# Splitting the first load of a row-variance kernel into 16 and 112 partitions

## The chip, the cores and the metric

The kernel runs on one core of one Trainium2 chip. The metric is the device time of one execution in microseconds (us); three runs of the kernel before the change had a median of 164.93 us (164.89 to 165.06).

## The reference

The input `x` is 32 x 512 rows of 1024 float32 numbers, 67.1 MB in all. For each row the kernel returns the mean of the squares minus the square of the mean, a single float32.

```python
def reference(x: np.ndarray) -> np.ndarray:
    mean_sq = np.mean(x**2, axis=-1)
    sq_mean = np.mean(x, axis=-1)**2
    return (mean_sq - sq_mean).astype(np.float32)
```

## The kernel before

The 16,384 rows are laid out as 128 partitions times 128 columns: partition p holds rows 128p to 128p + 127, each row being one "column" of 1024 elements. Sixteen columns make a tile. A tile is loaded by one DMA that brings 16 neighbouring rows, 64 KB (65,536 bytes) contiguous in memory, into each of the 128 partitions: 8.39 MB. Three slots in SBUF hold tiles in turn (`slots`, `SLOTS = 3`).

All loads go out on SyncE (SP), through the helper `load` at line 124 of the profile. `load` first puts waits for the slot to be free on SP (line 123) and then the DMA, which adds 16 to its semaphore when it has landed. The order is written out by hand:

- six main tiles (`MAIN`), one DMA each. Tiles 0, 1 and 2 fill the three slots with nothing to wait for; tile t from 3 on waits until VectorE (DVE) and ScalarE (ACT) are done with tile t - 3 (`freed`).
- the last two tiles in a taper of ever smaller DMAs (`TAPER`, 11 columns down to 1) and five pieces of half and quarter columns (`PIECES`).

Of a main tile, ten or eleven columns are taken by DVE, two `bn_stats` of 512 elements each (lines 128 and 130), and the other five or six by ACT, a Square and a Copy pass with an accumulator each (line 139). Both engines wait for the semaphore of the tile before their first column and for nothing else of the loads. GpSimd (POOL) folds the statistics into variances (lines 155 to 189) when a group is complete. The last pieces go through `bn_stats` and `bn_aggr` on DVE (lines 302 and 307), and one DMA stores all 16,384 results.

The kernel allocates its semaphores itself and runs inside one critical section. After the program is built, `move` takes the load of tile 0 (all DMAs whose names are in `early`) out of the section and puts it at the very start of SP's program, ahead of the barrier in which all engines meet (line 365 in the profile); the wait for the store is put at the end. The places that the change touches are the list `rows` in the loop over tiles, which names the partition ranges in which tile 0 is loaded, and what follows from it: one `load` for each entry, one name in `early` for each, and `landed = (tile_sems[t], 16 * len(rows))`, the value for which DVE and ACT wait.

Of the kernel before, what the change touches and what calls it, by code (L numbers as in the profile page):

```python
# [10 lines left out]
P = 128  # L11
# [27 lines left out]
    (127, 768, 256),  # L39
]  # L40

class Stream:
# [24 lines left out]
def kernel(  # L70
# [8 lines left out]
    def src(c, n, e0=0, elems=D, p0=0, np=P):  # L79
        return dataclasses.replace(  # L80
            xf,
            offset=(p0 * NCOLS + c) * D + e0,
            ap=[[NCOLS * D, np], [1, (n - 1) * D + elems]],
        )
# [27 lines left out]
    def slot(t):  # L112
        return slots[t % SLOTS]

    def column(t, j, e0=0, n=D):
        return slot(t)[:, j * D + e0 : j * D + e0 + n]
# [4 lines left out]
    def load(dst, source, sem, *waits):  # L121
        for s, v in waits:
            nc.sync.wait_ge(s, v)  # L123
        return nc.sync.dma_start(out=dst, in_=source).then_inc(sem, 16)  # L124

    def bn_column(stats, xcol, *waits):
        dve.issue(
            lambda: nc.vector.bn_stats(out=stats[:, 0, :], in_=xcol[:, 0:HALF]), *waits  # L128
        )
        return lambda: nc.vector.bn_stats(out=stats[:, 1, :], in_=xcol[:, HALF:D])  # L130
# [14 lines left out]
    def act_column(xcol, c, *waits):  # L145
        act_pass(xcol, ACTF.Square, 1.0 / 32.0, msq[:, c : c + 1], *waits)
        act_pass(xcol, ACTF.Copy, 1.0 / D, mv[:, 0, c : c + 1])
# [45 lines left out]
    with tc.tile_critical(no_gpsimd_drain=True):  # L193
# [4 lines left out]
        freed = []  # L198
        for t in range(MAIN):
            if t == 0:  # L200
                rows = [(0, P)]
            else:
                rows = [(0, P)]
            waits = freed[t - SLOTS] if t >= SLOTS else ()
            for p0, np in rows:
                ins = load(
                    slot(t)[p0 : p0 + np, :],
                    src(t * SLOT, SLOT, p0=p0, np=np),
                    tile_sems[t],
                    *waits,  # L210
                )
                if t == 0:
                    early.append(ins.ins.name)
            landed = (tile_sems[t], 16 * len(rows))
            first_d = first_a = (landed,)
            n_bn = MAIN_BN - (t < SPARE)
            for j in range(SLOT):
                if j < n_bn:
                    last = bn_column(stats_main[:, t * MAIN_BN + j], column(t, j), *first_d)
                    first_d = ()  # L220
                    if j == n_bn - 1:
                        dve.step(last)
                    else:
                        last()
                else:
                    act_column(column(t, j), t * SLOT + j, *first_a)
                    first_a = ()
            freed.append((dve.done(), act.done()))
# [141 lines left out]
```

## Time and profile before

| | |
|---|---|
| median of 3 runs | 164.93 us (164.89 to 165.06) |
| the profiled execution | 164.89 us |
| its span, first to last instruction | 162.4 us |
| what lies around the span | 2.5 us |
| DVE busy | 103.0 us (63%) |
| ACT busy | 91.7 us (56%) |
| POOL busy | 12.3 us (8%) |
| DMA, share of 16 engines' span | 96.7% on SP's queue |
| HBM read | 67.11 MB, 414 GB/s over the span |

Busy times overlap each other, as do consecutive instructions of one engine. Of the DMA there is one share for all 16 DMA engines together, and the bytes that they moved. In the tables by stretch a DMA packet is counted, with its bytes and its time, in the stretch in which it starts; one packet of a main tile's load is one partition's 64 KB. A very short stretch can therefore show a share far above 1 and a rate that no engine has: it says how many packets started there.

### The profile page before, as it was taken

The page shows a single profiled execution, that of the slowest core. Times are in us where ns is not written, and L with a number is a line of the kernel's source. Part 1 is how long each engine was busy: PE and PEld are TensorE (multiplying, and loading weights), DVE is VectorE, ACT ScalarE, POOL GpSimd, SP SyncE. Part 2 cuts the span into 40 slices and gives each one's busy share as a digit, 9 for nine tenths or more (in the row PEclk, how much of TensorE's full clock was granted, in tenths as well). Part 3 has the DMA queues.
Part 4 walks back from the last instruction along what each step waited for, and adds up shares of the span by engine and source line. Part 5 has one row for each costly group of instructions (what it writes and reads, how often), then busy time and mean ns, then how long its engine had stood idle before and what let it go on. Part 6 is the DMA issues. An engine that isn't in the chain of part 4 may idle for free.

```text
span 162.4 us, 476 instructions
## 1 busy us (share of the span) xinstructions
DVE 103.0 (63%) x175; ACT 91.7 (56%) x173; POOL 12.3 (8%) x51
## 2 busy tenths in 40 slices
DVE  0000049940799208993199913998059999999983
ACT  3000049960799308960199403992059939987990
POOL 0000000000000000000000000000000048300172
DMA  8998997997997998998998999899799999999980
GB/s 274 500 468 355 468 484 339 468 500 339 452 517 339 438 517 357 420 517 371 404 517 371 404 517 404 371 517 436 339 444 444 433 390 438 429 424 410 405 317 16
DMA packets 2738, 67.19 MB, mean 414 GB/s; under 512 B 304, under 2 KB 688, under 8 KB 1328
## 3 DMA queue, kind: packets, MB, share of 16 engines
q1 hardware_dynamic: 2736, 67.18, 96.7%
q14 instruction: 2, 0.02, 0.0%
HBM read 67.11 MB, written 0.07 MB: 414 GB/s over the span
## 4 chain that ended last, share of the span: by engine, by line
DMA 78%; DVE 10%; ACT 8%; SPq 2%; issue 0%
DMA slot<-in_x_dram 78%; ACT scratch L139 8%; DVE stats_main L128 4%; DVE stats_main L130 4%; SPq L124 2%; DVE stats_end L302 2%; DVE mv L307 0%; SPq L365 0%; SPq L123 0%; SPq L193 0%
## 5 line engine op out<-in xcount | busy, mean ns | idle before, releaser
L139 ACT ACTIVATE scratch<-slot 128x1024 f32<-128x1024 f32 x86 | 86.7, 1008 | 65.6 <-DMA slot<-in_x_dram 65.5
L128 DVE BATCH_NORM_STATS2 stats_main<-slot 128x6 f32<-128x512 f32 x64 | 43.4, 679 | 56.0 <-DMA slot<-in_x_dram 56.0
L130 DVE BATCH_NORM_STATS2 stats_main<-slot 128x6 f32<-128x512 f32 x64 | 43.3, 677 | 0.0
L139 ACT ACTIVATION_READ_ACCUMULATOR scratch<-slot 128x1 f32 x86 | 16.1, 187 | 0.0
L155 POOL TENSOR_TENSOR sqm<-mv 128x2 f32<-128x2 f32 (+3 forms) x8 | 1.6, 201 | 142.2 <-ACT scratch L139 142.2
L128 DVE BATCH_NORM_STATS2 stats_late<-slot 128x6 f32<-128x512 f32 x17 | 11.6, 682 | 0.4 <-DMA slot<-in_x_dram 0.2
L130 DVE BATCH_NORM_STATS2 stats_late<-slot 128x6 f32<-128x512 f32 x17 | 11.5, 677 | 0.0
L302 DVE BATCH_NORM_STATS2 stats_end<-slot 128x6 f32<-128x512 f32 (+1 forms) x5 | 2.7, 569 | 0.3 <-DMA slot<-in_x_dram 0.3
L139 ACT ACT_TABLE_LOAD x1 | 1.3, 1283 | 0.9 <-SPq L193 0.9
L156 POOL TENSOR_TENSOR mv<-msq,sqm 128x2 f32<-128x2 f32 (+3 forms) x8 | 1.6, 202 | 0.6
L130 DVE BATCH_NORM_STATS2 stats_end<-slot 128x6 f32<-128x512 f32 x2 | 1.4, 676 | 0.0
L128 DVE BATCH_NORM_STATS2 stats_end<-slot 128x6 f32<-128x512 f32 x2 | 1.3, 668 | 0.0
L189 POOL TENSOR_SCALAR mv<-qsb_late 128x7 f32<-128x7 f32 (+3 forms) x4 | 0.8, 238 | 0.1
L172 POOL TENSOR_TENSOR q_main<-stats_main 128x264 f32<-128x264 f32 x1 | 0.6, 642 | 2.1 <-DVE stats_main L130 2.1
L166 POOL TENSOR_TENSOR msa_main<-stats_main 128x132 f32<-128x132 f32 x1 | 0.6, 595 | 0.0
L166 POOL TENSOR_TENSOR vsa_main<-stats_main 128x132 f32<-128x132 f32 x1 | 0.6, 577 | 0.0
L307 DVE BATCH_NORM_AGGREGATE mv<-stats_end 128x2 f32<-128x12 f32 (+1 forms) x2 | 0.5, 225 | 0.1
L274 DVE BATCH_NORM_AGGREGATE mv<-stats_end 128x2 f32<-128x12 f32 x2 | 0.4, 211 | 0.1
L166 POOL TENSOR_TENSOR qsa_main<-q_main 128x132 f32<-128x132 f32 x1 | 0.4, 406 | 0.1
L178 POOL TENSOR_SCALAR msb_main<-msb_main 128x66 f32<-128x66 f32 x1 | 0.4, 404 | 0.1
L182 POOL TENSOR_SCALAR qsb_main<-qsb_main 128x66 f32<-128x66 f32 x1 | 0.4, 395 | 0.1
L189 POOL TENSOR_SCALAR mv<-qsb_main 128x66 f32<-128x66 f32 x1 | 0.4, 385 | 0.1
(23 smaller groups left out, 5.4 us busy)
## 6 DMA issues: line engine op xcount, KB each, us to landing
slot<-in_x_dram SPq DMA_DIRECT2D x1, 5632.0 KB, 38.8
slot<-in_x_dram SPq DMA_DIRECT2D x1, 3584.0 KB, 28.0
slot<-in_x_dram SPq DMA_DIRECT2D x1, 2560.0 KB, 33.7
slot<-in_x_dram SPq DMA_DIRECT2D x1, 1536.0 KB, 36.9
slot<-in_x_dram SPq DMA_DIRECT2D x1, 1024.0 KB, 38.9
slot<-in_x_dram SPq DMA_DIRECT2D x2, 512.0 KB, 40.1
slot<-in_x_dram SPq DMA_DIRECT2D x3, 256.0 KB, 40.6
slot<-in_x_dram SPq DMA_DIRECT2D x2, 128.0 KB, 28.6
```

The lines of the kernel that those rows point to most:

```text
L124: return nc.sync.dma_start(out=dst, in_=source).then_inc(sem, 16)
L128: lambda: nc.vector.bn_stats(out=stats[:, 0, :], in_=xcol[:, 0:HALF]), *waits
L130: return lambda: nc.vector.bn_stats(out=stats[:, 1, :], in_=xcol[:, HALF:D])
L139: lambda: nc.scalar.activation(out=row, in_=xcol, func=func, scale=scale, accum_out=accum),
L155: w = pool.step(lambda: tt(out=sqm, in0=mean, in1=mean, op=ALU.mult), *waits)
L156: pool.step(lambda: tt(out=var, in0=meansq, in1=sqm, op=ALU.subtract), w)
L166: lambda: tt(out=a, in0=v[:, :, 0:2], in1=v[:, :, 2:4], op=ALU.add), *waits
L172: w = pool.step(lambda: tt(out=q, in0=mean, in1=mean, op=ALU.mult), *waits)
L178: lambda: ts(out=ms, in0=ms, scalar1=0.25, scalar2=None, op0=ALU.mult), w
L189: lambda: ts(out=var, in0=qs, scalar1=1.0 / D, scalar2=None, op0=ALU.mult),
L302: lambda: nc.vector.bn_stats(out=stats[:, s, :], in_=dst), (piece_sems[i], 16)
L307: lambda: nc.vector.bn_aggr(out=mv[:, :, c], in_=stats[:, 0:s, :]), w
```

## The change

Tile 0 is loaded by two DMAs in place of one. The first brings the 16 columns of partitions 0 to 15 (1.05 MB), the second those of partitions 16 to 127 (7.34 MB). Both stand at the start of SP's program, ahead of the entry barrier, and both add 16 to the same semaphore, so that DVE and ACT wait for 32 instead of 16. Every other DMA and every instruction of the other engines is the same, in the same order.

```diff
@@ -39,7 +39,7 @@
     (127, 768, 256),
 ]
 
-
+FIRST = 16
 
 
 class Stream:
@@ -198,7 +198,7 @@
         freed = []
         for t in range(MAIN):
             if t == 0:
-                rows = [(0, P)]
+                rows = [(0, FIRST), (FIRST, P - FIRST)]
             else:
                 rows = [(0, P)]
             waits = freed[t - SLOTS] if t >= SLOTS else ()
```

## The prediction

> **What bounds the kernel now.** I read the page first, its slices and its chain.
>
> ```profile
> span 162.4 us, 476 instructions
> DMA  8998997997997998998998999899799999999980
> GB/s 274 500 468 355 468 484 339 468 500 339 452 517 339 438 517 357 420 517 371 404 517 371 404 517 404 371 517 436 339 444 444 433 390 438 429 424 410 405 317 16
> DMA 78%; DVE 10%; ACT 8%; SPq 2%; issue 0%
> ```
>
> The sixteen DMA engines are busy in every slice up to the last one or two, and 78% of the chain that ended last is loads of x. Where the chain runs through ACT (24 passes) or DVE, it follows the release of a slot back, not a stage in which the loads stood still. The waits, asked next, say the same from the engines' side:
>
> ```profile
> ACT scratch L139 <- DMA slot<-in_x_dram: 65.5, 9, 20.2
> DVE stats_main L128 <- DMA slot<-in_x_dram: 56.0, 6, 22.4
> DVE stats_end L302 <- DMA slot<-in_x_dram: 0.3, 1, 0.3
> DVE stats_late L128 <- DMA slot<-in_x_dram: 0.2, 1, 0.2
> ```
>
> DVE waits for a load at each of the six main tiles, 56.0 us together, and only 0.5 us after that. So up to the landing of tile 5 the loads set the pace, and then DVE keeps step with them.
>
> How a load runs is read from stretches cut for it: the start, the second row of each engine, and whole tiles.
>
> ```profile
> core 0: us, DVE busy (x) ACT busy (x) POOL busy (x), PEclk, DMA share, GB/s
> 0.00:0.90 0.90, 0.00 (x0) 0.00 (x0) 0.19 (x4) 1.00 0.00 0
> 0.90:1.10 0.20, 0.00 (x0) 0.16 (x1) 0.12 (x2) 1.00 6.09 1966
> 1.10:1.30 0.20, 0.00 (x0) 0.20 (x1) 0.04 (x1) 1.00 2.97 983
> 1.30:1.50 0.20, 0.00 (x0) 0.20 (x1) 0.00 (x0) 1.00 1.06 328
> 1.50:1.70 0.20, 0.00 (x0) 0.20 (x1) 0.00 (x0) 1.00 1.02 328
> 1.70:1.90 0.20, 0.00 (x0) 0.20 (x1) 0.00 (x0) 1.00 4.94 1638
> 1.90:3.90 2.00, 0.00 (x0) 0.32 (x1) 0.00 (x0) 1.00 0.00 0
> 3.90:6.40 2.50, 0.00 (x0) 0.00 (x0) 0.00 (x0) 1.00 0.97 419
> 22.40:41.70 19.30, 11.97 (x20) 12.58 (x24) 0.00 (x0) 1.00 1.00 435
> ```
>
> A packet counts where it starts. 1966 GB/s for 0.2 us is 0.393 MB, six packets of 64 KB; the next stretches hold 3, 1, 1 and 5, sixteen in all, then 2 us without a start, then 419 GB/s x 2.5 us = 1.05 MB, sixteen again. So each of 16 engines takes one partition's 64 KB at a time, one after the other. In steady running (22.4 to 41.7) they move 435 GB/s, 27.2 GB/s each: **one partition's 64 KB takes 2.41 us**, and a tile, eight partitions an engine, 19.3 us. Their first packets start over 0.9 us, between 0.9 and 1.9.
>
> **The change, part by part.**
>
> *The second issue on SP.* One more DMA issue stands ahead of the entry barrier. The issue instructions of line 124 last 0.33 to 0.44 us where nothing holds them up. On SP three things are behind it: its part in the barrier, tile 1's issue (at 0.98 us now) and all later loads. SP waits 0.7 us at line 365 for the others anyway, which covers it. Without that cover, tile 1's issue would come at 1.4, and its packets are wanted when tile 0's are through, near 20 us; DVE and ACT, released by the barrier, have nothing to do before 22.4. Cost: nothing, 0.4 us if it fell on the path. The wait for 32 instead of 16 costs nothing by itself: it is the same wait, ended by the later landing.
>
> *The 16-partition DMA.* It is sixteen packets of 64 KB, as many as the engines. The trace of before has no load on fewer than 128 partitions, so its price needs bounds. If the 2.41 us belong to the engine, sixteen engines take a packet each side by side: 2.41 us, the same as those rows cost now. If they belong to the way into a group of partitions, sixteen neighbouring partitions may reach only a few of the sixteen ways. The one ratio that the trace has is eight partitions to an engine: if those eight were neighbours with one way of their own, 16 partitions would be two ways, eight packets after one another on each: 19.3 us, so 16.9 us lost. Between the ends lie four ways (4 x 2.41 = 9.6 us, 7.2 lost) and eight ways (4.8 us, 2.4 lost). Below nothing is possible too: see the first rival. I take **four ways, +7.2 us**: the row that bears on it, eight partitions to an engine, points to the two-way end, and I go one halving away from it because the groups need not be of eight neighbours.
>
> Here the Trainium skill speaks against the change. "SBUF — State Buffer", section "Door 1: The DMA port swizzle", says that DMA rate depends on how many of 16 ports the partitions reach, that partitions 0 to 15 reach four, and gives 104 GB/s for 1 MiB on them. By that figure the first DMA would take an estimated 10.1 us and the sum would be about 173 us from this step alone; by the steady row of this trace, read as the engine's own, it would be unchanged. No run of before shows which.
>
> *The 112-partition DMA.* Seven packets an engine, 7 x 2.41 = 16.9 us if all sixteen run side by side; with the first DMA that is eight packets an engine, as now, so the low bound is 0. But if ways into partitions count, those that the first DMA did not use still have all their eight packets to take: 19.3 us, one packet time more. And with seven partitions an engine, shares no longer line up with groups of eight: in the worst case two engines share a way throughout, 16.9 us more. I take the value nearest to the steady row, which has eight packets on a way: **+2.4 us**.
>
> *Does it reach the end?* Between tiles the only thing DVE and ACT wait for is the load; DVE sits idle 6.2 to 7.6 us before the start of tiles 1 to 5. Tiles 1 and 2 stand in the same queue behind tile 0 and come later by as much. Slot 0 is free by the same amount later, but tile 3's DMA lies queued for long before it is served: the six main loads take 45.2 us from issue to landing, of which 19.3 is work. So a delay of tile 0 moves all landings, the taper and the tail as a block. The same holds for a gain.
>
> *Sum.* The profiled execution took 164.89 us, 162.4 of span and 2.5 around it, 0.04 under the median of 164.93. 164.9 + 0 + 7.2 + 2.4 = **174.5 us**.
>
> **The rivals.**
>
> *Faster: the engines start together.* Now the sixteen engines start over 0.9 us, and the landing of the tile is that of the last one. If the spread comes from laying out eight packets an engine, one packet each cuts it to an eighth, 0.11 us, and the last engine gains 0.8; if it comes from elsewhere, 0. Middle of the upper half: 0.6 us, **164.3 us**. It decides if the 2.41 us belong to the engine: then the 16-partition DMA has no price, and any gain at the start is left over. For it: sixteen separate starts, a late group of five at 1.7 to 1.9, and a rate that is the same for every packet. Against it: a steady 16 x 27.2 GB/s in loads over all partitions cannot tell engine and way apart. Chance 0.25.
>
> *Two ways, or heavy sharing in the second DMA.* Two ways give +16.9, with one packet time more +19.3: 181.8 to **184.2 us**. Four ways with 4 to 5 packet times lost in the 112-partition DMA come to the same. For it: the ratio of eight to an engine. Against it: it needs the worst layout. Chance 0.2.
>
> *Nothing moves.* Engine-bound packets and a start spread that the split leaves alone: **164.9 us**. The bytes, the engines and the order are the same, so this is what the change not doing what it says looks like. Chance 0.05.
>
> *Only the issue costs.* Engine-bound, but the second DMA's packets come 0.4 us late or its engines restart: **165.3 us**. Against it: the first DMA's 2.41 us cover the 0.4. Chance 0.05.
>
> **How the numbers follow.** The forecast case, a few ways shared, has 0.45; its own range goes from eight ways and nothing more (167.3) to four ways and two packet times (177). Faster 0.25, same 0.05, slower 0.45 + 0.2 + 0.05 = 0.70; 0.2% (0.33 us) is about what a measurement of this kernel can tell from no change. The range starts at the largest gain, 164.1, since the faster case alone is more than may be left out, and ends at 183, inside the two-way case, with some 0.1 above it.
>
> **What would show it.** In the changed profile the 16-partition DMA takes near 10 us to land rather than 3 to 4, the rate in the first 10 us falls to a quarter of 435 GB/s, DVE's first wait goes from 22.4 to near 32 us, and all later landings shift by the same 9.6 us with 19.3 us between them. It is wrong if the second sixteen packets start at 3.9 to 6.4 us as now: then the engine sets the rate, and what is left is the start. If the gap between the first and second landing is not 19.3 us, the engines were left uneven, and the 112-partition term is mis-sized.

## The result, and the profile after

The changed kernel takes **185.59 us** (median of 4 runs, 185.47 to 185.84) where the kernel before takes 165.0 (4 runs, 164.89 to 165.1): the ratio is 1.125, with a 95% interval of 1.1231 to 1.127. It is 20.6 us slower. The forecast was 174.5 us, and its range ended at 183: the sign was right, the size was not. The profiled execution has a span of 183.3 us against 162.4.

The page of the changed kernel, the lines that answer to those shown of before:

```profile
span 183.3 us, 477 instructions
DMA  9199999977899999998899999999899999999970
GB/s 229 29 200 229 343 300 229 229 229 329 386 458 443 458 458 458 431 443 388 372 443 443 458 458 458 443 415 415 386 429 452 442 391 423 425 426 403 409 286 17
DMA 71%; ACT 14%; DVE 9%; another core or an unknown queue 4%; SPq 2%; issue 0%
```

Read the share and the GB/s line together. The share of the DMA engines is as high as before, 96.7% over the span, but in the first nine slices (4.6 us each) they move some 200 to 340 GB/s in place of 435. They are not idle. Their packets last longer. (The single 1 and the 29 in the second slice come from counting a packet where it starts.) From the twelfth slice on the rate is that of before. The chain has more of ACT, whose 24 passes it now follows in two tiles, and a 6.7 us piece, from 56.3 to 63.05 us, that it could not place; tile 1's load was running then.

The waits:

```profile
ACT scratch L139 <- DMA slot<-in_x_dram: 86.1, 9, 41.0
DVE stats_main L128 <- DMA slot<-in_x_dram: 77.1, 6, 43.7
DVE stats_end L302 <- DMA slot<-in_x_dram: 0.3, 1, 0.3
DVE stats_late L128 <- DMA slot<-in_x_dram: 0.2, 1, 0.2
```

DVE's longest wait, the one for tile 0, went from 22.4 to 43.7 us. The sum went from 56.0 to 77.1, so the other five waits together are as they were (33.6 and 33.4), and so is the 0.5 us after them. The whole loss is in the landing of tile 0, and it is passed on as a block: the taper's first column starts on DVE at 153.77 us against 132.74, 21.0 later.

The start, in stretches that are cut at the packets' starts:

```profile
core 0: us, DVE busy (x) ACT busy (x) POOL busy (x), PEclk, DMA share, GB/s
0.90:1.90 1.00, 0.00 (x0) 0.49 (x1) 0.15 (x2) 1.00 8.51 1049
1.90:8.70 6.80, 0.00 (x0) 0.80 (x1) 0.00 (x0) 1.00 0.00 0
8.70:10.50 1.80, 0.00 (x0) 0.00 (x0) 0.00 (x0) 1.00 3.10 583
10.50:14.70 4.20, 0.00 (x0) 0.00 (x0) 0.00 (x0) 1.00 0.00 0
14.70:43.30 28.60, 0.00 (x0) 0.00 (x0) 0.00 (x0) 1.00 1.01 259
43.70:63.00 19.30, 11.97 (x20) 12.58 (x24) 0.00 (x0) 1.00 1.00 435
```

1049 GB/s for 1 us and 583 for 1.8 are sixteen packets of 64 KB each: the first packets (the 16-partition DMA) start between 0.9 and 1.9 us, and the second ones between 8.7 and 10.5. In a row with sixteen starts, one for each engine, the share times the row's length is the mean time of one packet: 8.5 us for the first packets, 5.6 for the second. The row with 259 GB/s also counts the first packets of tile 1; up to 39.7 us, without them, it is 252. Before, the second ones started between 4.0 and 5.2:

```profile
1.90:4.00 2.10, 0.00 (x0) 0.32 (x1) 0.00 (x0) 1.00 0.00 0
4.00:5.20 1.20, 0.00 (x0) 0.00 (x0) 0.00 (x0) 1.00 2.03 874
5.20:20.00 14.80, 0.00 (x0) 0.00 (x0) 0.00 (x0) 1.00 0.98 425
```

So the 16-partition DMA cost the last engine 5.3 us (10.5 against 5.2), and the 112-partition DMA the rest: 43.7 - 10.5 = 33.2 us against 22.4 - 5.2 = 17.2, **16.0 us more**. 5.3 + 16.0 = 21.3, the shift of the landing. From 43.7 on a tile takes 19.3 us at 435 GB/s again.

### The profile page after: what moved, and what is told of

Its sections match the earlier page's. It is cut to its first block, busy times and chain, and to the rows that moved or that the text cites. A ratio compares the mean times of both kernels' runs of the same rounds, so it can differ in the third digit from the quotient of the medians.

```text
span 183.3 us, 477 instructions
## 1 busy us (share of the span) xinstructions
DVE 102.9 (56%) x175; ACT 91.7 (50%) x173; POOL 12.3 (7%) x51
## 3 DMA queue, kind: packets, MB, share of 16 engines
q1 hardware_dynamic: 2752, 67.18, 96.7%
## 4 chain that ended last, share of the span: by engine, by line
DMA 71%; ACT 14%; DVE 9%; another core or an unknown queue 4%; SPq 2%; issue 0%
DMA slot<-in_x_dram 71%; ACT scratch L139 14%; DVE stats_main L128 4%; DVE stats_main L130 4%; SPq L124 2%; DVE stats_end L302 1%; DVE mv L307 0%; SPq L123 0%
## 5 line engine op out<-in xcount | busy, mean ns | idle before, releaser
L128 DVE BATCH_NORM_STATS2 stats_main<-slot 128x6 f32<-128x512 f32 x64 | 43.4, 678 | 77.1 <-DMA slot<-in_x_dram 77.1
```

## The experiments

Theory A is that partitions reach SBUF through sixteen ways of limited rate, that a DMA over part of the partitions reaches only some of them or lets two engines meet on one, and that the sharing is the whole loss. In every kernel but one, marked below, the load of tile 0 is the only thing that differs from the kernel before. "Before" beside them was 164.88 to 165.04 us. Where no ratio is given, the time is that of one execution.

**Two DMAs, split by columns.**

```diff
-                rows = [(0, P)]
+                rows = [(0, 2), (2, SLOT - 2)]
...
-                    slot(t)[p0 : p0 + np, :],
-                    src(t * SLOT, SLOT, p0=p0, np=np),
+                    slot(t)[:, k0 * D : (k0 + nk) * D],
+                    src(t * SLOT + k0, nk),
```

> Tile 0 in two DMAs, but split by columns: 2 of 16 columns for all 128 partitions, then 14 columns for all 128. Theory A (what costs is that 16 neighbouring partitions, and seven-partition shares after them, share few ways into SBUF): no such sharing, so 165.0 us, within 0.4 us either way. Rival B (what costs is a second DMA for the same tile, a restart or a completion between the two): most of the 20.6 us stays, 180 us or more. If the first engines' starts come closer together, a gain of up to 0.8 us.

Measured: 164.73 us against 164.92, ratio 0.9991 (0.9982 to 1.0); DVE waits 22.0 us for tile 0. A second DMA for the tile, a second issue ahead of the barrier and the wait for 32 cost nothing. Rival B falls.

**Eight DMAs of 16 neighbours.**

```diff
-                rows = [(0, P)]
+                rows = [(16 * i, 16) for i in range(8)]
```

> Tile 0 in eight DMAs of 16 neighbouring partitions each. Theory A: each takes what the first DMA of the changed kernel took, 8 to 9.7 us, so tile 0 takes 64 to 77 us in place of 19.3 and the kernel 210 to 223 us. Rival B (each further DMA costs the same fixed time, 20.6 us for one): seven further ones, 309 us. If only the seven-partition shares of the 112-partition DMA were slow: 165 us plus little.

Measured: 218.57 us. Past the first DMA, the stretches show the rate of the remaining ones and then of tile 1:

```profile
10.60:76.00 65.40, 0.00 (x0) 0.00 (x0) 0.00 (x0) 1.00 0.90 112
76.30:95.60 19.30, 12.01 (x21) 12.62 (x25) 0.00 (x0) 1.00 1.00 435
```

112 GB/s on sixteen neighbouring partitions, 435 on all: about a quarter, as four ways of sixteen would give. The packets there last 9.18 us each. (Such long rows, here and below, also count tile 1's first packets, which moves them by 2% at most: 114 GB/s without them.)

**The same, with every eighth partition.**

```diff
-                rows = [(0, P)]
+                rows = [(i, 16) for i in range(8)]
...
-                    slot(t)[p0 : p0 + np, :],
+                    slot(t)[p0 : p0 + (np - 1) * step + 1 : step, :],
```

The source rows follow with the same step of 8.

> Tile 0 in eight DMAs of 16 partitions again, but every eighth partition: 0, 8, 16 ... 120, then 1, 9, ... in destination and source alike. Theory A: sixteen partitions spread over the whole range reach more ways. If a way serves eight neighbours, all sixteen: 165 us. If groups of four are dealt over eight of the ways, two packets to a way: 4.8 us a DMA, 38.6 us for the tile, 184 us. Rival B and any theory of the number of partitions or DMAs: as with eight DMAs of neighbours.

Measured: 186.43 us, in the second of theory A's two cases, 2.4 over its figure. Same number of DMAs, packets and bytes as in the kernel with neighbours, and 32 us less:

```profile
7.80:43.00 35.20, 0.00 (x0) 0.00 (x0) 0.00 (x0) 1.00 0.95 207
```

207 GB/s is about half of 435, packets of 5.11 us, eight ways. Which partitions a DMA names sets its rate, not how many. Nor can a way belong to eight neighbours: every eighth partition would then have a way of its own, and the full rate.

**The source alone.** The destinations are the eight groups of 16 neighbours again; only the rows that are read change.

```diff
+                own = dict(p0=p0 // 16, step=8) if t == 0 else dict(p0=p0)
                 ins = load(
                     slot(t)[p0 : p0 + np, :],
-                    src(t * SLOT, SLOT, p0=p0, np=np),
+                    src(t * SLOT, SLOT, np=np, **own),
```

> Eight DMAs, destination 16 neighbouring partitions as in the first kernel of this kind, but the source rows are those of every eighth partition, so tile 0 holds rows in another order and its results belong to other rows. Theory A (ways into the destination): the same time as with neighbours on both sides, 210 to 223 us. Rival C (the reading side: neighbouring partitions' rows, 512 KB apart in memory, collide): the time of the kernel with every eighth partition on both sides.

Measured: 220.8 us, 2.2 more than with neighbours on both sides.

```profile
10.60:76.00 65.40, 0.00 (x0) 0.00 (x0) 0.00 (x0) 1.00 0.96 111
```

The rate stays at 111 GB/s while the rows read are those of the kernel that ran at 207. The limit is on the destination; rival C falls. (A spread destination filled from neighbouring rows was not run.)

**The two parts the other way round.**

```diff
-                rows = [(0, P)]
+                rows = [(0, 112), (112, 16)]
```

> The same two sizes the other way round: partitions 0 to 111 first, then 112 to 127. Theory A (the 112-partition DMA is slow by itself, since seven neighbours to an engine make two engines share a way): the 112 take about the 31 us that they took in the changed kernel, the 16 then 9.2 us, in all 180 to 187 us. Rival D (the 112-partition DMA was slow because the 16-partition DMA left the engines out of step): the 112 take near 17 us, and the kernel about 172 us.

Measured: 185.38 us.

```profile
0.00:6.00 6.00, 0.00 (x0) 1.28 (x1) 0.34 (x6) 1.00 1.24 295
6.00:32.70 26.70, 0.00 (x0) 0.00 (x0) 0.00 (x0) 1.00 1.15 248
29.80:32.70 2.90, 0.00 (x0) 0.00 (x0) 0.00 (x0) 1.00 2.94 362
32.70:42.40 9.70, 0.00 (x0) 0.00 (x0) 0.00 (x0) 1.00 0.41 108
```

The 112 partitions, first in the queue now, are through at 32.7 us, near 32 after the first packet; at 27.2 GB/s an engine they would take 16.9. The packets of the 16 partitions are the sixteen that start between 29.8 and 32.7, and they last 8.5 us each on average. The last row has none of them: its sixteen starts are tile 1's first packets, so its 108 GB/s is not their rate. The 112-partition DMA is slow by itself; rival D falls.

**64 and 64 partitions, 32 and 96.**

```diff
-                rows = [(0, P)]
+                rows = [(0, 64), (64, 64)]
```

> Two equal parts of 64 partitions, four packets an engine in each. If an engine takes four neighbours and 64 neighbouring partitions reach eight ways, every way has two engines throughout: 8 packets x 5.11 us (the pace of two to a way in the run with every eighth partition) = 40.9 us for the tile, 186.4 us in all. If an engine takes every sixteenth partition, four engines share a way: 8 x 9.18 = 73.4 us, 219 us. If the odd number of seven partitions was the fault: 165 us.

```diff
-                rows = [(0, P)]
+                rows = [(0, 32), (32, 96)]
```

> Parts of 32 and 96 partitions, two and six packets an engine. Theory A: 32 neighbours reach eight ways, 2 x 5.11 = 10.2 us; in the 96 each six-partition share starts in one group of four and ends in the next, so that most packets share a way at some time; between 6 x 2.41 = 14.5 and 6 x 5.11 = 30.7 us, nearer to the upper end as with seven. In all 25 to 41 us for the tile, 171 to 187 us, most likely 183.

Measured: 186.03 and 184.9 us, near theory A's figures (186.4, and 183 as the likeliest). The kernel with 64 and 64, behind the first two packets of each engine:

```profile
7.00:42.60 35.60, 0.00 (x0) 0.00 (x0) 0.00 (x0) 1.00 0.96 208
```

It is 208 GB/s throughout, and each packet in the steady part lasts 4.95 to 5.13 us, the pace of two engines to a way in the run with every eighth partition. Seven partitions an engine are not the fault, since four cost the same. By the expectation, an engine that took every sixteenth partition would have given 219 us.

**Tile 1 split in place of tile 0.**

```diff
-            if t == 0:
+            if t == 1:
-                rows = [(0, P)]
+                rows = [(0, 16), (16, P - 16)]
```

> Tile 0 whole, tile 1 split into 16 and 112 partitions; its DMAs are issued after the entry barrier and served in mid-stream. Theory A (sharing of ways, wherever it happens): the same loss, 184 to 187 us, and DVE's wait for tile 0 back at 22.4 us. Rival E (the loss belongs to the start: the cold queue, or issues ahead of the barrier): 165 us.

Measured: 187.93 us, 23.0 slower. DVE starts tile 0 at 24.27 us (22.43 before) and tile 1 at 65.11, 40.8 us later where it was 19.3. The loss does not belong to the start; rival E falls. It is even 2.4 us larger, of which 1.8 is tile 0's later landing, though that tile is loaded whole. The expectation of 22.4 us for DVE's first wait was wrong. Tile 0's last packets last up to 3.2 us while engines that finished first are already on the 16-partition DMA; they end 0.6 us later than before, and DVE starts 1.7 us after the last of them in place of 0.4. A collision on the ways would fit, but it was not tested apart.

**How the price grows.** The next kernels split only the first 2 or 8 of tile 0's columns into 16 and 112 partitions, and then all 16 columns two at a time. An entry of `rows` has the first partition, the number of partitions, the first column and the number of columns.

```diff
-                rows = [(0, P)]
+                rows = [(0, 16, 0, 2), (16, P - 16, 0, 2), (0, P, 2, SLOT - 2)]
```

> Only the first 2 of tile 0's 16 columns are loaded in 16 and 112 partitions; the other 14 come whole. Theory A (a price for every byte that goes through a shared way): 2/16 of 20.6 us = 2.6 us, 167.5 us. Rival B (a price for each DMA on part of the partitions): near 185 us. If small packets hide the sharing: 165 us.

```diff
-                rows = [(0, P)]
+                rows = [(0, 16, 0, 8), (16, P - 16, 0, 8), (0, P, 8, 8)]
```

> The first 8 of 16 columns in 16 and 112 partitions (packets of 32 KB), the other 8 whole. Theory A, a price for each byte sent through a shared way: half of 20.6 us, 175.2 us. If what two columns cost (0.8 us) is the price of an amount of bytes, 4 x 0.8 = 3.2 us, 168.1 us. A price that begins only after a first stretch of each DMA lies between.

```diff
-                rows = [(0, P)]
+                rows = [(p, n, k, 2) for k in range(0, SLOT, 2) for p, n in ((0, 16), (16, P - 16))]
```

> All 16 columns in 16 and 112 partitions, but two columns at a time: sixteen DMAs of 16 or 112 packets of 8 KB, the same bytes into the same partitions as in the changed kernel. Theory A, a price for each byte: 185 us again. Rival F (a long packet holds its engine at a shared way, short ones let the engines drift past each other): 8 x 0.8 = 6.4 us, 171 us.

Measured: 165.67 us (+0.8; ratio 1.0049, 1.0034 to 1.0063), 173.08 (+8.0 over 165.04) and 176.16 (+11.1). A price for each byte alone, theory A in its plain form, would be 2.6, 10.3 and 20.6 us. In pairs of columns the same bytes go into the same partitions at a higher rate:

```profile
1.00:32.00 31.00, 0.00 (x0) 1.28 (x1) 0.15 (x2) 1.00 1.01 270
```

By the start of its first packet and the end of its last, tile 0 takes 31.5 us here (266 GB/s) and 41.9 in the changed kernel (200). In packets of 8 KB the split cost about half of what it cost in packets of 64 KB. But it is not the 6.4 us that rival F expected either: the first pair cost 0.8 us and the eight together 11.1, so a first stretch is cheap. Neither account is right alone. The pairs also send the 16 and the 112 partitions in turn, so the length of the packets is not the only thing that changed; why they lose less was not settled.

**Can the split be turned into a gain?** One, two and four columns first, always on 128 partitions; the edit is that of the first experiment with another number.

> Tile 0 by columns again, 1 of 16 columns for all partitions and then 15. If the small gain with two columns (164.73 us) is real and comes from small first packets that let all engines start together, about the same, 164.6 to 164.8 us; if it was noise, 164.9 us. No theory has it near 180 us.

> Tile 0 by columns, 4 and then 12, both on all 128 partitions. No theory has a cost; a gain from engines that start together, if there is one, gives 164.6 to 164.8 us, and 164.9 us otherwise.

> The split by 2 and 14 columns once more, to see whether its 164.73 us against 164.92 is a gain: 164.7 us with the interval of the ratio below 1 if it is, 164.9 us if not.

Measured: one column 164.85 us against 164.88 (ratio 0.9995, 0.9986 to 1.0004); four columns 164.66 against 164.89 (0.9989, 0.9981 to 0.9998); two columns again 164.81 against 164.89 (0.9993, 0.9984 to 1.0003). All lean to the fast side, one interval only lies wholly below 1, and the best is 0.2 us. Four columns first is the fastest kernel of the study, by 0.1%, less than the bound of 0.2% set in the prediction.

## Why the prediction was wrong in size

*What bounds the kernel* held: the loads do, and what tile 0 lost arrived at the end nearly whole (21.3 us at its landing, 20.9 in the span, 20.6 in the medians). *Does it reach the end?* was right.

*The second issue* at nothing was right: the split by columns has it and is no slower.

*The 16-partition DMA*, +7.2 on four ways: the ways are four (112 of 435 GB/s), and the measured cost is 5.3 us. The first packet lasted 3 us and more before, not 2.41, so less was there to lose; and sixteen neighbours ran at 28 GB/s a way, a little over the 27.2 of an engine. The reason given for four was weak, one halving away from the only ratio in the trace, so that it came out right was luck. Here the Trainium skill had the number. "SBUF — State Buffer", section "Door 1: The DMA port swizzle", gives 104 GB/s for partitions 0 to 15 and four ports; this case has 112. Its table and formula also put eight ports under partitions 0 to 63, eight under 64 to 127, and eight under every eighth partition; the runs have 208 and 207 GB/s.

*The 112-partition DMA* is **the step that failed: +2.4 us in the sum, +16.0 measured**. The prediction had named what could happen, and the end of the bound: shares no longer line up with the groups, two engines share a way throughout, "16.9 us more". It then took the value "nearest to the steady row, which has eight packets on a way". That row is the one case in which every engine has a way of its own, so it says nothing about shares that straddle groups. Every split of tile 0 into two by partitions, 16 and 112, 112 and 16, 64 and 64, 32 and 96, cost 20.0 to 21.2 us, about a second 19.3. With 64 and 64, every packet keeps the pace of two engines to a way. The seven packets that an engine has in the 112-partition DMA last 5.6, 4.8, 3.2, 3.8, 4.5, 4.7 and 4.5 us on average, where the sum had allowed one packet time of 2.41 more in all. The second and the third of them in the changed kernel, sixteen starts to a row:

```profile
14.70:15.70 1.00, 0.00 (x0) 0.00 (x0) 0.00 (x0) 1.00 4.78 1049
19.50:20.40 0.90, 0.00 (x0) 0.00 (x0) 0.00 (x0) 1.00 3.54 1165
```

All sixteen engines slow down together (4.75 to 4.91 us in the second packet, 2.75 to 4.75 in the third, the most uneven one), none keeps the 2.42 of an engine with a way of its own, and only the first packets, which overlap those of the 16-partition DMA, take longer than the 5.11 of two to a way. So the size is measured, and the swapped order shows that the DMA is slow by itself; that shares of seven meet on ways is argued. The traces do not name the partition of a packet, and why all sixteen slow down together stays open.

*The rivals.* The "heavy sharing in the second DMA" case, four ways with 4 to 5 packet times lost in the 112-partition DMA, came nearest: it named 181.8 to 184.2 us and had a chance of 0.2. Even so it was too small, since 16.0 us are 6.6 packet times. The range was then cut at 183, inside that case, when four ways (7.2) and the upper bound of the second DMA (16.9) together already gave 189. *Engines start together* fell: the starts did come closer in part (fifteen of sixteen first packets by 1.4 us), but the destination, not the engine, set the length of a packet. What may be left of that idea is the 0.0 to 0.2 us of the split by columns. *What would show it* held in part: the rate of the first packets fell to about a quarter and the second packets no longer start at 3.9 to 6.4 us, but DVE's first wait went to 43.7 us and not to 32. The sign named for a mis-sized 112-partition term, a gap between the first two landings that is not 19.3 us, stayed away: the gap is 19.3 (DVE starts tile 0 at 43.74 us, tile 1 at 63.07), and the term was mis-sized all the same, since its whole price lies ahead of the first landing.

The skill's warning in "DMA: Bandwidth & Descriptors", section "Rules for kernel authors", that two transfers to disjoint partition halves serialize and one over all 128 should be used, agrees with the runs: 64 and 64 took 21.2 us more. The rule of the same section that wants the outermost dimension a multiple of 16, so that all 16 engines are used, is kept by 16 and by 112: all sixteen engines took part, and the loss came all the same.

## What to carry to other kernels

Where loads set the pace, as here, split a load along the bytes of a partition rather than along the partitions: one, two or four columns first on all 128 partitions cost nothing, while splitting a tile into two by partitions cost about as much as loading it again (20.0 to 23.0 us), and eight groups of neighbours 53.7. Only a split of its first two columns was cheap, 0.8 us. When a trace holds only full-width transfers, its rate cannot tell an engine's limit from a destination's, and a term bounded from 0 to 16.9 us belongs in the range with both ends, however plausible its low end. Busy DMA engines are no sign of a full rate: read the GB/s line beside the share.

## What the runs showed of the hardware

Sixteen neighbouring partitions take data at 111 or 112 GB/s, sixteen spread by eight or 64 neighbours at 207 or 208, all 128 at 435; spreading the source rows alone did not raise the rate. Not expected were four things. At half the rate, read as two engines to a way, a packet takes 5.11 us, 6% more than twice 2.41, while at a quarter, read as four, it takes 9.18, 5% less than four times. In the 112-partition DMA all sixteen engines slow down together, to 3.2 to 4.8 us a packet on average behind the first. The same bytes cost less in shorter packets sent in turn: 11.1 us with 8 KB, 20.6 with 64 KB. And a split in mid-stream cost 2.4 us more than at the start, of which 1.8 is the later landing of the whole tile ahead of it.
